# A hybrid pooling and state-space block on one core: the TensorE order of the gate and pooling projections is written out as 64 steps

## The chip, the core and the metric

The kernel runs on one core of a Trainium2 chip. The metric is the device time of one execution in microseconds (us). Before the change the median of three runs is 1359.53 us (1359.49 to 1359.74).

The engines are called as in the profile: PE is the matrix engine (TensorE), PEld its weight loads, DVE the vector engine, ACT the scalar engine with its table functions, POOL the third elementwise engine, SP the engine that issues most DMAs. Each engine runs its own list of instructions in order and waits on semaphores for the others.

## The reference

One layer of a decoder. Two request groups share the weights: 256 prompt tokens and 8 x 4 sample tokens, so 288 columns (N) everywhere. D_MODEL is 2048, that is 16 blocks of 128 (KT).

```python
mod = silu(c) @ w_ada + b_ada                  # six parts: sh1, sc1, g1, sh2, sc2, g2
h = rmsnorm(x, norm1) * (1 + sc1) + sh1
u_pool, z, xbc, dt_raw = split(h @ w_in)       # widths 512, 1536, 2560, 24
pool_out = pool_mixer(u_pool)                  # trailing windows 2/4/8/16, then a 128x128 map per group
ssd_out = ssd_mixer(z, xbc, dt_raw)            # conv of width 4, chunked scan, y * silu(z), rmsnorm
x = x + g1 * (concat([pool_out, ssd_out]) @ w_out)
h2 = rmsnorm(x, norm2) * (1 + sc2) + sh2
x = x + g2 * conv_ffn(h2)                      # gate and value projections, conv of width 3, down projection
y = rmsnorm(x, norm_f)
```

Inside the state-space mixer (SSD) each of four groups has six heads of 64 channels and a state of 128:

```python
Lm = exp(where(mask, cs[l] - cs[s], -inf))                    # decays, per head
y_diag = (C B^T * Lm) @ xdt;  y_off = (C * exp(cs)) @ h_start
chunk_states = (B * decay_to_end)^T @ xdt
```

## The kernel before

Activations are kept transposed, 128 features by 288 tokens a tile. Every large projection is done in three matmuls for one block of weights (`mm3`, lines 295 to 297): the weights are cast on ACT into a rounded high part (`whi`), DVE subtracts to get the low part (`wlo`), and PE adds high x high, high x low and low x high. These matmuls use all 128 columns of the PE array and stream 288 columns; the text calls them **wide**. The wide names are `xbc`, `mm_uz`, `mm_out`, `mm_up`, `mm_gate`, `mm_val` and `mm_down`.

The weights come as one stream of tiles of up to 512 KB, loaded by SP in the order in which the program asks for them into eight `raw` buffers (`RAW0`).

Three kinds of PE work use only part of the array's columns at a time, the text calls them **narrow**: the conditioning matmuls `adap` (32 columns each, four side by side, line 324), `yo` (32 columns) and the SSD outputs `y` (64 columns, two side by side, lines 807 to 817). A float32 matmul stands as two records in the trace, so 8 matmuls of `adap` are 16 records.

The stage that the change is about is the projection of the gate z and of two pooling groups, `uz_units(m)` for eight tiles m. A tile is 16 blocks of the contraction; `project_units` yields every two of them (`YK`), so the stage has 64 steps of six wide matmuls. Between the steps other work is pulled from generators:

- `adas` is the conditioning for parts 2, 3 and 4 of `mod`. One unit of `ada_part_units` (`AY` = 2 blocks) needs four weight tiles and eight `adap` matmuls. The text calls that a **visit**. After a part's eight visits come a copy on ACT (`asb`) and four transposes (`adat`).
- `back` is the SSD. `ssd_group(g)` transposes tokens (`xt`, `bt`), forms C B^T (`cb`), chunk states (`s`), the sample part `yo`, and then for each of three head pairs t the decays `decays(t)` (two matmuls `cse`, six relus and two exps on ACT, one exp over both heads, two products on DVE) and `outputs(t)` (ten matmuls `y`, then DVE and ACT). `conv_group(g)` is the convolution of the next group, 15 DVE operations and a SiLU.
- `late` and `pool_units` are the pooling mixer, `y_norm` the norm of the SSD output: column sums `ysum`, a square root on ACT, a reciprocal on DVE, the matmuls `pbrstdy`, and three products on DVE and one on POOL over the four `zy` tiles.

`pull(gn, rate)` adds the rate to a credit and takes a unit from the generator for every whole credit. In this stage the rates are 0.2 visits and one SSD unit a step. What is pulled is only traced there: the framework's scheduler then orders each engine's instructions by its own estimates, so a visit or a group of `y` may be cut and wide matmuls put between its parts. The block `in_order(...)` (it adds a dependence from each instruction to the one before on the named engines) is used before the change only for the first stage of the kernel.

PSUM for `xt`, `bt`, `cb`, `s`, `yo`, `cse`, `y`, `pool` and `adat` comes from four `aux` banks in turn.

After the stage follows the output projection `mm_out`. Its right-hand sides `mixh` and `mixl` are made on ACT and DVE from the normed `zy` and the pooling output; the first tile can go no faster than they appear.

Of the kernel before, what the change touches and what calls it, by code (L numbers as in the profile page):

```python
# [18 lines left out]
P = 128  # L19
# [31 lines left out]
GB = 4  # L51
AY = 2

RA1, RA2, RB1, RB2, RB3 = 0.5, 0.4, 1.0, 1.0, 1.0
TA, ADA_OUT = 4, 4
TK = 4
GA = (2, 3)
XM = (0, 2, 5, 9)
SM0 = 10
# [102 lines left out]
def kernel(ctx: ExitStack, tc, ins, outs):  # L162
# [14 lines left out]
    def aux(name):  # L177
        return px.tile([P, 512], F32, tag="aux", name=name)
# [80 lines left out]
    def load(key):  # L259
        off, cols = S.items[key]  # L260
        t = wp[0].tile([P, RAWC], F32, tag="raw", name="raw_" + "_".join(map(str, key)))
        nc.sync.dma_start(t[:, :cols], wflat[off:off + P * cols].rearrange("(p n) -> p n", p=P))
        return t
# [54 lines left out]
        return ps  # L318


    def ada_mm(ps, raw, k, c0, nb, js):
        for j in js:
            c = c0 + (j - js[0]) * nb
            nc.tensor.matmul(ps[32 * j:32 * j + 32, :nb], sc_c[:, k, :], raw[:, c:c + nb],  # L324
                             start=(k == 0), stop=(k == KT - 1), tile_position=(0, 32 * j))

    def ada_sb(ps, nb, name, r=P):
        asb = kp.tile([P, 512], F32, tag="asb", name="asb_" + name)
        nc.scalar.copy(asb[0:r, :nb], ps[0:r, :nb])
# [66 lines left out]

    def ada_part_units(part, ay=1):
        ps = pa.tile([P, 512], F32, tag="ada", name=f"adap{part}")
        for k in range(KT):
            raws = [load(("adap", part, k, h)) for h in range(2)]  # L400
            for h in range(2):
                ada_mm(ps, raws[h], k, 0, 512, range(2 * h, 2 * h + 2))
            if k % ay == ay - 1:
                yield
        asb = ada_sb(ps, 512, f"p{part}")
        yield
        pt = ada_tr(asb, 512, f"p{part}")
        for i in range(4):
            o = ada[:, part].rearrange("p (j i) c -> p j i c", j=4)[:, :, i, :]
            b = bada[:, part].rearrange("p (j i) -> p j i", j=4)[:, :, i]  # L410
            src = pt[:, i * P:(i + 1) * P].rearrange("p (j c) -> p j c", j=4)[:, :, 0:NC9]
            nc.vector.tensor_tensor(o, src, b.unsqueeze(2).to_broadcast([P, 4, NC9]), ALU.add)
        if part == 4:
            ada_scale(1, 4, vec[:, V_N2:V_N2 + KT], 0, KT)
        yield
# [237 lines left out]
    def drain(gen):  # L653
        for _ in gen:
            pass
# [54 lines left out]
    def ssd_group(g):  # L710
# [35 lines left out]
        nc.gpsimd.dma_start(sbx[q, P:P + G6], xde[0:NS, 2, :])  # L746
        yield

        s1 = sx[0].tile([P, G6], F32, tag="s1", name=f"s1_{g}")
        ps1 = aux(f"s1_{g}")  # L750
        nc.tensor.matmul(ps1[:, :G6], bt[:, 0, :], xde[:, 0, :], start=True, stop=True)
# [24 lines left out]
                                py[:, :G6].rearrange("p (h q) -> p h q", h=HG),  # L776
                                bc64(dtr["ecs4"][:, hs]), ALU.mult)
        yield

        csr, cs = dtr["csr"], dtr["cs"]  # L780

        def decays(t):

            e = sx[0].tile([P, 2, N], F32, tag="e", name=f"e{g}_{t}", bufs=2)
            ec = sx[0].tile([P, 2, P], F32, tag="ec", name=f"ec{g}_{t}", bufs=2)
            for i in range(2):
                hh = HG * g + 2 * t + i
                pe = aux(f"cse{hh}")
                nc.tensor.matmul(pe[:, :N], selr[:, hh:hh + 1].to_broadcast([P, P]), csr, start=True, stop=True)


                for c in range(3):
                    n = slice(c * P, min(c * P + P, N))
                    nc.scalar.activation(e[:, i, n], pe[:, n], AF.Relu, bias=cs[:, c, hh:hh + 1], scale=-1.0)
                nc.scalar.activation(ec[:, i, :], pe[:, P:NP], AF.Exp)
            nc.scalar.activation(e, e, AF.Exp, scale=-1.0)
            nc.vector.tensor_tensor(e, e, cb.unsqueeze(1).to_broadcast([P, 2, N]), ALU.mult)
            nc.vector.tensor_tensor(ec, ec, cf[:, 4, P:NP].unsqueeze(1).to_broadcast([P, 2, P]), ALU.mult)
            return e, ec

        def outputs(t, e, ec):
            assert (g, t) in zdone
            pq = aux(f"y{g}_{t}")
            rows = [slice(0, 64), slice(64, P)]
            for i, r in enumerate(rows):
                f = slice(64 * (2 * t + i), 64 * (2 * t + i) + 64)
                nc.tensor.matmul(pq[r, NP:N], yo[:, f], seli, start=True, stop=False)
            for i, r in enumerate(rows):
                f = slice(64 * (2 * t + i), 64 * (2 * t + i) + 64)
                nc.tensor.matmul(pq[r, NP:N], xdt[:, 2, f], e[:, i, NP:N], start=False, stop=True)  # L810
            for i, r in enumerate(rows):
                f = slice(64 * (2 * t + i), 64 * (2 * t + i) + 64)
                nc.tensor.matmul(pq[r, 0:P], xdt[:, 0, f], e[:, i, 0:P], start=True, stop=True)
            for i, r in enumerate(rows):
                f = slice(64 * (2 * t + i), 64 * (2 * t + i) + 64)
                nc.tensor.matmul(pq[r, P:NP], xdt[:, 1, f], e[:, i, P:NP], start=True, stop=False)
                nc.tensor.matmul(pq[r, P:NP], s1[:, f], ec[:, i, :], start=False, stop=True)
            yt = cf[:, t, 0:N]
            nc.vector.scalar_tensor_tensor(out=yt, in0=yt,
                                           scalar=vec[:, V_D + 3 * g + t:V_D + 3 * g + t + 1],  # L820
                                           in1=pq[:, :N], op0=ALU.mult, op1=ALU.add)
            zt = zy[g][:, t, :]
            nc.vector.tensor_tensor(zt, zt, yt, ALU.mult)
            sq = kp.tile([P, N], F32, tag="xsq", name=f"ysq{g}_{t}", bufs=2)
            nc.scalar.activation(sq, zt, AF.Square)
            if g + t == 0:
                nc.gpsimd.tensor_copy(ssq, sq)
            else:
                nc.gpsimd.tensor_tensor(ssq, ssq, sq, ALU.add)

        if g < ZEARLY:
            nc.scalar.activation(zy[g], zy[g], AF.Silu)
        dec = [decays(0)]
        yield
        dec.append(decays(1))
        outputs(0, *dec[0])
        yield
        dec.append(decays(2))
        outputs(1, *dec[1])
        yield  # L840
        outputs(2, *dec[2])
# [61 lines left out]
    def chain(*gens):  # L903
        for gn in gens:
            yield from gn
# [50 lines left out]
    def zip2(a, b):  # L956
        a, b = iter(a), iter(b)
        live = 2
        while live:
            live = 0  # L960
            for gn in (a, b):
                try:
                    next(gn)
                    live += 1
                    yield
                except StopIteration:
                    pass

    def h0s(g):
        load_h0(g)  # L970
        yield

    def take(gn, n):
        for _ in range(n):
            next(gn)
            yield

    ssd3 = ssd_group(3)
    back = chain(conv0, h0s(0), zip2(ssd_group(0), conv_group(1)), h0s(1),
                 zip2(ssd_group(1), conv_group(2)), h0s(2), zip2(ssd_group(2), conv_group(3)), h0s(3),  # L980
                 zip2(take(ssd3, TK), chain(pool_units(UEARLY[0]), pool_units(UEARLY[1]))))
    credit = {}

    def pull(gn, rate):

        credit[id(gn)] = credit.get(id(gn), 0.0) + rate
        while credit[id(gn)] >= 1:
            credit[id(gn)] -= 1
            next(gn, None)
# [29 lines left out]
                pull(back, 0.5 if m < 20 else RB1) if m >= 9 else None  # L1019
                pull(adas, RA1 / AY)  # L1020

    late = {}
    n = 0
    zlast = 3 * (4 - ZEARLY) * KT // YK
    for m in list(range(4 + 3 * ZEARLY, 16)) + ULATE:
        for _ in uz_units(m):
            n += 1
            for gn in late.values():
                pull(gn, 0.5)
            pull(adas, RA2 / AY)  # L1030
            pull(back, RB2 if n <= zlast else RB3)
            if n == zlast:
                drain(back)
                back = chain(ssd3, y_norm())
        if m < 4:
            late[m] = pool_units(m)
            next(late[m])
    pull(adas, TA / AY)
    for h, (_, n) in enumerate(_halves(KT)):
        ready[("out", 0, h)] = split(load(("out", 0, h)), 0, n * P, f"out_0_{h}")  # L1040
    for gn in late.values():
        drain(gn)
    drain(back)
    npl = kp.tile([P, 4, 135], F32, tag="hmod", name="npl", bufs=2)
    nc.gpsimd.tensor_copy(npl[:, :, 0:15], upp[:, :, NP:15 + NP])
    nc.gpsimd.tensor_copy(npl[:, :, 15:135].rearrange("p g (b l) -> p g b l", b=NB), ups[:, :, :, 4:19])
# [63 lines left out]
    for m in range(16):  # L1110
        if m in XM:
            sl = slice(4 * XM.index(m), 4 * XM.index(m) + 4)
            nc.sync.dma_start(x[:, sl, :], ins["x"][:, sl, :])
        if m == 5:
            wp[0].add(w2, RAW2, SPLIT2)
        for i, ps in enumerate(project_units(("out", m), KT, order=MIXK)):
            if m == KT - 1 and i == 5:
                all_but_last("ssum2")
        residual(ps, 2, m)
        squares(m, "a")  # L1120
        pull(adas, (1 + (m >= 14 - ADA_OUT)) / AY)
        if m == 13:
            drain(adas)

# [286 lines left out]
```

## Time and profile before

| | |
|---|---|
| median of 3 runs | 1359.53 us |
| the profiled execution's own time | 1359.61 us |
| its span, first to last instruction | 1357.8 us |
| mean granted PE clock | 0.997 |
| PE busy in the span | 1342.5 us, 99% |
| first `mm_dt` matmul | 186.3 us |
| first `mm_uz` matmul | 260.93 us |
| first `mm_out` matmul | 380.34 us |

All times on the trace are us from the start of the span. A matmul is recorded with its full latency, so a wide one shows about 0.30 us though the next starts 0.13 us later; what a matmul takes of PE's time is the distance from its start to the next start. PE shows as busy nearly always, also where it streams at a lower pace, so its busy share doesn't tell how much could be gained. ACT and DVE records overlap a little as well.

### The profile page before, as it was taken

Reading aid. Unit: us, or ns where it says so; the run is one execution under the profiler, and the core shown is the slowest. Engines: PE = TensorE matmul, PEld = TensorE weight load, DVE = VectorE, ACT = ScalarE, POOL = GpSimd, SP = SyncE. Lnnn points to the kernel's source line nnn. Section 1 sums busy time; section 2 is a strip of 40 time slices with the busy share of each in tenths; the row PEclk is TensorE's granted clock in tenths of the full one; section 3 lists DMA queues with packets and bytes.
Section 4 is the critical chain, followed back from the end, with each engine's and each line's share of the span. In section 5 each row is a group of like instructions: output and inputs, shape, how many; then the busy total and the mean of one; then the engine's idle time right before and its main releaser. Section 6 shows DMA issues by size and latency. Waiting matters only on the chain.

```text
span 1357.8 us, 26226 instructions
## 1 busy us (share of the span) xinstructions
PE 1342.5 (99%) x10557; PEld 1247.4 (92%) x10557; DVE 810.1 (60%) x1349; ACT 578.6 (43%) x908; POOL 221.0 (16%) x428
## 2 busy tenths in 40 slices
PE   9999999999999999999999999999999999999997
PEld 7889988776779889999999999999999999999996
DVE  5775568778564448645565455656654556566543
ACT  5243234587643335534443334443433344434442
POOL 0000002122221213111221001212220011222221
PEclk9999999999999999999999999999999999999998
DMA  9999668877888877777555455555554555555531
GB/s 378 405 408 355 252 216 323 335 263 288 326 302 334 310 265 257 248 293 265 184 182 184 167 176 185 197 193 182 189 178 167 183 191 185 192 200 194 180 117 71
DMA packets 97338, 323.20 MB, mean 238 GB/s; under 512 B 10752, under 2 KB 19904, under 8 KB 97216
## 3 DMA queue, kind: packets, MB, share of 16 engines
q1 hardware_dynamic: 93312, 310.64, 62.8%
q0 software_dynamic: 3184, 9.69, 1.9%
q8 instruction: 83, 1.36, 0.4%
q10 hardware_dynamic: 720, 1.19, 0.2%
q14 instruction: 39, 0.32, 0.1%
HBM read 309.78 MB, written 10.39 MB: 236 GB/s over the span
## 4 chain that ended last, share of the span: by engine, by line
PE 96%; DVE 2%; DMA 1%; ACT 0%; issue 0%; SPq 0%; POOL 0%; DVEq 0%; POOLq 0%; ACTq 0%
PE mm_down L296 7%; PE mm_down L295 7%; PE mm_down L297 7%; PE mm_val L296 6%; PE mm_gate L296 6%; PE mm_gate L295 6%; PE mm_gate L297 6%; PE mm_val L297 6%; PE mm_val L295 6%; PE xbc L295 5%; PE adap L324 5%; PE xbc L296 4%; PE xbc L297 4%; PE mm_out L295 3%; PE mm_out L296 3%; PE mm_out L297 2%
## 5 line engine op out<-in xcount | busy, mean ns | idle before, releaser
L296 PE MATMUL mm_down<-al,whi_down 128*128 128x288 f32 x688 | 202.9, 295 | 0.0
L295 PE MATMUL mm_down<-ah,whi_down 128*128 128x288 f32 x688 | 202.7, 295 | 0.0
L297 PE MATMUL mm_down<-ah,wlo_down 128*128 128x288 f32 x688 | 202.4, 294 | 0.0
L296 PE MATMUL mm_gate<-h2l,whi_gate 128*128 128x288 f32 x640 | 189.1, 296 | 0.0
L296 PE MATMUL mm_val<-h2l,whi_val 128*128 128x288 f32 x640 | 189.1, 295 | 0.0
L297 PE MATMUL mm_val<-h2h,wlo_val 128*128 128x288 f32 x640 | 188.8, 295 | 0.0
L297 PE MATMUL mm_gate<-h2h,wlo_gate 128*128 128x288 f32 x640 | 188.8, 295 | 0.0
L295 PE MATMUL mm_gate<-h2h,whi_gate 128*128 128x288 f32 x640 | 188.7, 295 | 0.0
L295 PE MATMUL mm_val<-h2h,whi_val 128*128 128x288 f32 x640 | 187.9, 294 | 0.0
L283 DVE TENSOR_TENSOR wlo_gate<-raw_gate,whi_gate 128x1024 fp32r<-128x1024 f32 x80 | 97.8, 1225 | 135.4 <-ACT whi_gate L281 135.2
L283 DVE TENSOR_TENSOR wlo_down<-raw_down,whi_down 128x1024 fp32r<-128x1024 f32 x96 | 107.5, 1119 | 116.1 <-ACT whi_down L281 115.0
L281 ACT CAST whi_down<-raw_down 128x1024 fp32r<-128x1024 f32 x96 | 92.4, 962 | 167.3 <-PE mm_down L296 118.0
L281 ACT CAST whi_gate<-raw_gate 128x1024 fp32r<-128x1024 f32 x80 | 83.9, 1051 | 159.5 <-PE mm_gate L296 67.7
L281 ACT CAST whi_val<-raw_val 128x1024 fp32r<-128x1024 f32 x80 | 84.1, 1051 | 126.0 <-issue 103.1
L295 PE MATMUL xbc<-h1h,whi_xbc 128*128 128x288 f32 x448 | 133.0, 301 | 1.2 <-ACT h1h L445 1.2
L296 PE MATMUL xbc<-h1l,whi_xbc 128*128 128x288 f32 x448 | 132.1, 296 | 0.0
L297 PE MATMUL xbc<-h1h,wlo_xbc 128*128 128x288 f32 x448 | 130.8, 297 | 0.0
L295 PEld LDWEIGHTS mm_down<-ah,whi_down 128*128 128x128 f32 x688 | 129.3, 188 | 0.0
L296 PEld LDWEIGHTS mm_down<-al,whi_down 128*128 128x128 f32 x688 | 129.3, 188 | 0.0
L297 PEld LDWEIGHTS mm_down<-ah,wlo_down 128*128 128x128 f32 x688 | 129.1, 188 | 0.0
L295 PEld LDWEIGHTS mm_gate<-h2h,whi_gate 128*128 128x128 f32 x640 | 120.5, 188 | 5.0 <-ACT ah L1176 3.4
L295 PEld LDWEIGHTS mm_val<-h2h,whi_val 128*128 128x128 f32 x640 | 120.5, 188 | 0.0
(323 smaller groups left out, 2979.3 us busy)
## 6 DMA issues: line engine op xcount, KB each, us to landing
raw_adap<-wflat SPq DMA_DIRECT2D x128, 512.0 KB, 5.5
raw_gate<-wflat SPq DMA_DIRECT2D x80, 512.0 KB, 3.5
raw_val<-wflat SPq DMA_DIRECT2D x80, 512.0 KB, 3.6
raw_ada<-wflat SPq DMA_DIRECT2D x64, 512.0 KB, 9.7
raw_xbc<-wflat SPq DMA_DIRECT2D x51, 512.0 KB, 8.9
raw_down<-wflat SPq DMA_DIRECT2D x48, 512.0 KB, 3.5
raw_out<-wflat SPq DMA_DIRECT2D x32, 512.0 KB, 6.6
raw_down<-wflat SPq DMA_DIRECT2D x32, 384.0 KB, 3.0
```

The source lines that it names most:

```text
L281: yield nc.scalar.copy(hi[:, :n], raw[:, a:a + n])
L283: yield hi, lo, nc.vector.tensor_tensor(lo[:, :n], raw[:, a:a + n], hi[:, :n].bitcast(F32), ALU.subtract)
L295: nc.tensor.matmul(ps, whi[:, w], bh, start=first, stop=False)
L296: nc.tensor.matmul(ps, whi[:, w], bl, start=False, stop=False)
L297: nc.tensor.matmul(ps, wlo[:, w], bh, start=False, stop=last)
L324: nc.tensor.matmul(ps[32 * j:32 * j + 32, :nb], sc_c[:, k, :], raw[:, c:c + nb], start=(k == 0), stop=(k == KT - 1), tile_position=(0, 32 ...
```

## The change

The generator rates of the stage go, and a plan takes their place: a list of what is pulled at which of the 64 steps. PE's instructions of the stage are put into `in_order`, so that PE has them as they are written. A visit's loads are all asked for first, and its matmuls are tied to each other from the last loaded tile on. In `ssd_group` the decays of the first head pair are made before the chunk states, each group's ten `y` matmuls are written as pairs over the two column halves, and the decays `e` and `ec` get a third buffer. Visits in the output projection are pulled at 5/7 a tile. What is computed stays the same.

```diff
-RA1, RA2, RB1, RB2, RB3 = 0.5, 0.4, 1.0, 1.0, 1.0
-TA, ADA_OUT = 4, 4
-TK = 4
+RA1, RB1 = 0.5, 1.0
+TA, ADA_OUT = 2, 5 / 7
+SSD0 = 4
+GA0, GP, GS = -6, 15, (0, 2, 3, 5, 6, 9, 12, 15)
+GCV, GH0 = (1, 2, 3, 4, 5, 6), 9
+VU = (3, 4, 6, 9, 18, 24, 33, 39, 48, 54, 61)
+YN = (58, 60)
+PU = (24, 28, 33, 34, 36, 39)
+PL = (58, 62)
...
     def ada_part_units(part, ay=1):
         ps = pa.tile([P, 512], F32, tag="ada", name=f"adap{part}")
-        for k in range(KT):
-            raws = [load(("adap", part, k, h)) for h in range(2)]
-            for h in range(2):
-                ada_mm(ps, raws[h], k, 0, 512, range(2 * h, 2 * h + 2))
-            if k % ay == ay - 1:
-                yield
+        for ka in range(0, KT, ay):
+            raws = [(k, h, load(("adap", part, k, h))) for k in range(ka, ka + ay) for h in range(2)]
+            tied = False
+            for k, h, raw in raws[::-1]:
+                for j in (2 * h, 2 * h + 1):
+                    with tc.high_priority() if tied else nullcontext():
+                        i = nc.tensor.matmul(ps[32 * j:32 * j + 32, :512], sc_c[:, k, :],
+                                             raw[:, (j % 2) * 512:(j % 2) * 512 + 512],
+                                             start=(k == ay - 1), stop=(k == KT - ay), tile_position=(0, 32 * j))
+                    if tied:
+                        tc.keep_in_program_order(i)
+                    tied = True
+            yield
...
+            e = sx[0].tile([P, 2, N], F32, tag="e", name=f"e{g}_{t}", bufs=3)
+            ec = sx[0].tile([P, 2, P], F32, tag="ec", name=f"ec{g}_{t}", bufs=3)
...
+            prods = [(P, NP, lambda i: (s1[:, fs[i]], ec[:, i, :]), True, False),
+                     (P, NP, lambda i: (xdt[:, 1, fs[i]], e[:, i, P:NP]), False, True),
+                     (0, P, lambda i: (xdt[:, 0, fs[i]], e[:, i, 0:P]), True, True),
+                     (NP, N, lambda i: (xdt[:, 2, fs[i]], e[:, i, NP:N]), True, False),
+                     (NP, N, lambda i: (yo[:, fs[i]], seli), False, True)]
+            for n0, n1, ops, first, last in prods:
+                for i, r in enumerate(rows):
+                    nc.tensor.matmul(pq[r, n0:n1], *ops(i), start=first, stop=last)
...
+    for g in range(4):
+        if g:
+            for i in range(3 if g == 1 else 0, 6):
+                at(GA0 + GP * (g - 1) + GCV[i], convs[g])
+            at(GA0 + GP * (g - 1) + GH0, h0s(g))
+        for i in range(SSD0 if g == 0 else 0, 8):
+            at(GA0 + GP * g + GS[i], ssds[g])
+    for n in VU:
+        at(n, adas)
+    for gn, steps in ((early_pool, PU), (yn, YN), (late[ULATE[0]], PL)):
+        for n in steps:
+            at(n, gn)
...
+    with in_order(nc.tensor.engine):
+        n = 0
+        step(0)
+        for m in list(range(4 + 3 * ZEARLY, 16)) + ULATE:
+            for _ in uz_units(m):
+                n += 1
+                if n % (KT // YK):
+                    step(n)
+            if m < 4:
+                next(late[m])
+            step(n)
+    pull(adas, TA)
```

**PE, the first tile of the stage.** The rows of before run from the second half of the visit with weight tiles 14 and 15 of part 2 through the first and second head pair of group 0 (`y_0`, `y_1`):

```order
L324 MATMUL adap_2522<-raw_adap_14_0_3278,sc_c 32x512 x2
L324 MATMUL adap_2522<-raw_adap_14_1_3280,sc_c 32x512 x2
L324 MATMUL adap_2522<-raw_adap_15_0_3286,sc_c 32x512
L810 MATMUL y_0_3240<-e_0_3190,xdt_2986 64x32 x2
L813 MATMUL y_0_3240<-e_0_3190,xdt_2986 64x128 x2
L816 MATMUL y_0_3240<-e_0_3190,xdt_2986 64x128
L817 MATMUL y_0_3240<-ec_0_3191,s_0_3116 64x128
L324 MATMUL adap_2522<-raw_adap_15_0_3286,sc_c 32x512
L324 MATMUL adap_2522<-raw_adap_15_1_3288,sc_c 32x512 x2
L789 MATMUL cse_3296<-csr,selr 128x288
...
L807 MATMUL y_1_3311<-vec,yo_3140 64x32 x2
L295 MATMUL mm_uz_3176<-h1h_123,whi_uz_1_3268 128x288
```

The same work in the changed kernel, the group `y_0` and the visit with tiles 14 and 15:

```order
L795 MATMUL y_0_3250<-ec_0_3118,s_0_3168 64x128 x2
L795 MATMUL y_0_3250<-e_0_3117,xdt_2986 64x128 x4
L795 MATMUL y_0_3250<-e_0_3117,xdt_2986 64x32 x2
L795 MATMUL y_0_3250<-vec,yo_3192 64x32 x2
L769 MATMUL cse_3268<-csr,selr 128x288
L769 MATMUL cse_3274<-csr,selr 128x288
L409 MATMUL adap_2522<-raw_adap_15_1_3295,sc_c 32x512 x2
L409 MATMUL adap_2522<-raw_adap_15_0_3293,sc_c 32x512 x2
```

The visit is no longer cut by `y_0`, and the product with `yo`, which stood apart from its group, is its last pair. Over the whole program PE's list has, from the first `mm_dt` to the first `mm_up`, 77 unbroken runs of wide matmuls before and 52 after (in the stage itself 48 and 26).

**PE, the norm of the SSD output near the end of the stage.** Before, wide matmuls stand between the column sums and the matmuls that spread the result:

```order
L296 MATMUL mm_uz_4305<-h1l_144,whi_uz_1_4449 128x288
L235 MATMUL ysum<-ones,ssq 128x1 x3
L297 MATMUL mm_uz_4305<-h1h_128,wlo_uz_1_4451 128x288
L295 MATMUL mm_uz_4507<-h1h_113,whi_uz_0_4510 128x288
...
L296 MATMUL mm_uz_4507<-h1l_135,whi_uz_0_4510 128x288
L248 MATMUL pbrstdy<-early,r3rstdy 128x128 x2
L248 MATMUL pbrstdy<-early,r3rstdy 128x32
L297 MATMUL mm_uz_4507<-h1h_119,wlo_uz_0_4512 128x288
```

Left out there are 18 further wide rows of `mm_uz`. In the changed kernel the two follow at once:

```order
L305 MATMUL mm_uz_4474<-h1l_132,whi_uz_0_4477 128x288
L306 MATMUL mm_uz_4474<-h1h_116,wlo_uz_0_4479 128x288
L244 MATMUL ysum<-ones,ssq 128x1 x3
L257 MATMUL pbrstdy<-early,r3rstdy 128x128 x2
L257 MATMUL pbrstdy<-early,r3rstdy 128x32
L304 MATMUL mm_uz_4474<-h1h_117,whi_uz_0_4477 128x288
```

What moved is the wide work that stood between them; it is now ahead and behind.

**ACT, the start of the stage.** Before, the two casts of the first tile's weights, `whi_uz_0` and `whi_uz_1`, stand ahead of all decays:

```order
L281 CAST whi_uz_0_3179<-raw_uz_0_3177 128x1024
L832 ACTIVATE zy_150<-zy_150 128x864
L281 CAST whi_uz_1_3268<-raw_uz_1_3266 128x1024
L794 ACTIVATE e_0_3190<-cse_3192,csd 128x128 x2
L794 ACTIVATE e_0_3190<-cse_3192,csd 128x32
L795 ACT_TABLE_LOAD
L795 ACTIVATE ec_0_3191<-cse_3192 128x128
```

In the changed kernel the second cast stands behind the decays of the second head pair (`e_1`, the rows before these) and inside those of the third (`e_2`):

```order
L776 ACTIVATE e_1_3194<-e_1_3194 128x576
L695 ACT_TABLE_LOAD
L695 ACTIVATE cf_3020<-cf_3020 128x5x32
L803 ACTIVATE ysq_0_3263<-zy_149 128x288
L774 ACTIVATE e_2_3266<-cse_3268,csd 128x128 x2
L290 CAST whi_uz_1_3315<-raw_uz_1_3313 128x1024
L774 ACTIVATE e_2_3266<-cse_3268,csd 128x32
L775 ACT_TABLE_LOAD
```

ACT's list has 20 table loads before and 28 in the changed kernel, because exps and SiLUs alternate more often; between the first `mm_uz` and the square root of the norm there are 14 before and 19 after.

More of the change, by code (lines that the diff above doesn't have):

```diff
@@ L318, in project @@
         return ps
[L321 to L325, printed above, removed]
     def ada_sb(ps, nb, name, r=P):
@@ L747, in ssd_group, with decays @@
         yield
+        csr, cs = dtr["csr"], dtr["cs"]
+        def decays(t):
+            e = sx[0].tile([P, 2, N], F32, tag="e", name=f"e{g}_{t}", bufs=3)
+            ec = sx[0].tile([P, 2, P], F32, tag="ec", name=f"ec{g}_{t}", bufs=3)
+            for i in range(2):
+                hh = HG * g + 2 * t + i
+                pe = aux(f"cse{hh}")
+                nc.tensor.matmul(pe[:, :N], selr[:, hh:hh + 1].to_broadcast([P, P]), csr, start=True, stop=True)
+                for c in range(3):
+                    n = slice(c * P, min(c * P + P, N))
+                    nc.scalar.activation(e[:, i, n], pe[:, n], AF.Relu, bias=cs[:, c, hh:hh + 1], scale=-1.0)
+                nc.scalar.activation(ec[:, i, :], pe[:, P:NP], AF.Exp)
+            nc.scalar.activation(e, e, AF.Exp, scale=-1.0)
+            nc.vector.tensor_tensor(e, e, cb.unsqueeze(1).to_broadcast([P, 2, N]), ALU.mult)
+            tc.keep_in_program_order(nc.vector.tensor_tensor(
+                ec, ec, cf[:, 4, P:NP].unsqueeze(1).to_broadcast([P, 2, P]), ALU.mult))
+            return e, ec
@@ new lines, in outputs @@
+        def outputs(t, e, ec):
+            assert (g, t) in zdone
+            pq = aux(f"y{g}_{t}")
+            rows = [slice(0, 64), slice(64, P)]
+            fs = [slice(64 * (2 * t + i), 64 * (2 * t + i) + 64) for i in range(2)]
+            prods = [(P, NP, lambda i: (s1[:, fs[i]], ec[:, i, :]), True, False),
[6 more added lines that the diff above has]
+                    nc.tensor.matmul(pq[r, n0:n1], *ops(i), start=first, stop=last)
+            yt = cf[:, t, 0:N]
+            nc.vector.scalar_tensor_tensor(out=yt, in0=yt,
+                                           scalar=vec[:, V_D + 3 * g + t:V_D + 3 * g + t + 1],
+                                           in1=pq[:, :N], op0=ALU.mult, op1=ALU.add)
+            zt = zy[g][:, t, :]
+            nc.vector.tensor_tensor(zt, zt, yt, ALU.mult)
+            sq = kp.tile([P, N], F32, tag="xsq", name=f"ysq{g}_{t}", bufs=2)
+            nc.scalar.activation(sq, zt, AF.Square)
+            if g + t == 0:
+                nc.gpsimd.tensor_copy(ssq, sq)
+            else:
+                nc.gpsimd.tensor_tensor(ssq, ssq, sq, ALU.add)
@@ L749, in ssd_group @@
+        if g < ZEARLY:
+            nc.scalar.activation(zy[g], zy[g], AF.Silu)
+        dec = [decays(0)]
+        yield
         s1 = sx[0].tile([P, G6], F32, tag="s1", name=f"s1_{g}")
@@ L778, in ssd_group @@
         yield
[L780 to L829, printed above, removed]
@@ L831, in ssd_group @@
-        if g < ZEARLY:
-            nc.scalar.activation(zy[g], zy[g], AF.Silu)
-        dec = [decays(0)]
+        dec.append(decays(1))
         yield
-        dec.append(decays(1))
         outputs(0, *dec[0])
+        dec.append(decays(2))
         yield
-        dec.append(decays(2))
         outputs(1, *dec[1])
@@ L976, in take @@
             yield
[L978 to L981, printed above, removed]
+    ssds = [ssd_group(g) for g in range(4)]
+    convs = [conv0] + [conv_group(g) for g in range(1, 4)]
+    back = chain(conv0, h0s(0), zip2(take(ssds[0], SSD0), take(convs[1], 3)))
     credit = {}
@@ L1020, with at, step @@
                 pull(adas, RA1 / AY)
[L1022 to L1038, printed above, removed]
+    drain(back)
+    yn = y_norm()
+    early_pool = chain(pool_units(UEARLY[0]), pool_units(UEARLY[1]))
+    late = {m: pool_units(m) for m in ULATE}
+    plan = [[] for _ in range(4 * KT + 1)]
+    def at(n, gn):
+        plan[max(n, 0)].append(gn)
+    for g in range(4):
[10 more added lines that the diff above has]
+            at(n, gn)
+    def step(n):
+        for gn in plan[n]:
+            next(gn, None)
+    with in_order(nc.tensor.engine):
[10 more added lines that the diff above has]
+    pull(adas, TA)
     for h, (_, n) in enumerate(_halves(KT)):
@@ L1042 @@
         drain(gn)
-    drain(back)
+    drain(yn)
     npl = kp.tile([P, 4, 135], F32, tag="hmod", name="npl", bufs=2)
@@ L1120 @@
         squares(m, "a")
-        pull(adas, (1 + (m >= 14 - ADA_OUT)) / AY)
+        pull(adas, ADA_OUT)
         if m == 13:
```

## The prediction

> **What bounds the kernel now.** I read the page first: busy shares and the chain that ended last.
>
> ```profile
> PE 1342.5 (99%) x10557; PEld 1247.4 (92%) x10557; DVE 810.1 (60%) x1349; ACT 578.6 (43%) x908; POOL 221.0 (16%) x428
> PE 96%; DVE 2%; DMA 1%; ACT 0%; issue 0%; SPq 0%; POOL 0%; DVEq 0%; POOLq 0%; ACTq 0%
> ```
>
> PE sets the time nearly everywhere, so a change pays only if PE streams with fewer losses or waits less. The chain is an average, so next came the view by windows of the stage, first the whole of it, then 15 of its steps (PE, PEld, DVE, ACT, POOL busy, clock, DMA share, GB/s), and PE's waits in the stage.
>
> ```profile
> 261.00:380.30 119.30, 117.57 (x948) 84.65 (x948) 85.35 (x159) 88.71 (x198) 27.64 (x37) 1.00 0.80 296
> 301.20:326.50 25.30, 25.30 (x219) 17.60 (x222) 20.23 (x39) 21.24 (x47) 6.66 (x11) 1.00 0.80 293
> PE pool L877 <- DVE pout L872: 0.7, 1, 0.7
> PE cse L789 <- DVE ada L412: 0.5, 1, 0.5
> PE cb L739 <- DVE xde L728: 0.4, 1, 0.4
> PE ysum L235 <- POOL ssq L829: 0.2, 1, 0.2
> ```
>
> Waits are 1.8 us of 119.3. Clock 1.00 and DMA share 0.80 leave no other bound. But ACT is busy 88.7 us (74%), and 21.2 of 25.3 us (84%) in the middle: a second engine stands close behind. What is left to gain lies in how PE streams, which the timeline of PE shows (start, length, what).
>
> ```profile
> 300.46 0.29 PE L296 MATMUL mm_uz<-h1l,whi_uz 128*128 128x288 f32 x1
> 300.69 0.31 PE L807 MATMUL y<-vec,yo 128*64 128x32 f32 x4
> 300.93 0.40 PE L297 MATMUL mm_uz<-h1h,wlo_uz 128*128 128x288 f32 x1
> 301.17 0.29 PE L295 MATMUL mm_uz<-h1h,whi_uz 128*128 128x288 f32 x1
> 301.30 0.29 PE L296 MATMUL mm_uz<-h1l,whi_uz 128*128 128x288 f32 x1
> ```
>
> From start to start a wide matmul takes 0.13 us (301.17 to 301.30), but 0.23 before a narrow group (300.46 to 300.69) and 0.24 as the first behind one (300.93 to 301.17). **A break costs 0.10 + 0.10 = 0.20 us.**
>
> The second loss is in the visits. The chain of waits shows a whole one and, first and last of eight, cut ones:
>
> ```profile
> 202.71 0.98 PE adap L324 x2
> 208.65 1.85 PE adap L324 x14
> 220.72 1.85 PE adap L324 x16
> ...
> 502.69 0.98 PE adap L324 x2
> 504.44 2.71 PE adap L324 x22
> ```
>
> Whole, 16 records take 1.85 us; cut into 2 and 14 they take 0.98 + 1.85 = 2.83, as much as half a visit more. The last pair holds a visit and a half: 3.69 against 1.5 x 1.85 = 2.78.
>
> **The change part by part.** The sum is made against the profiled execution's 1359.61 us; the median, 1359.53, is practically the same.
>
> *A. Visits tied.* In the new order no visit is cut. Eight times 0.97 = 7.8 us. Nothing hides this, since PE has no idle time there.
>
> *B. Fewer breaks.* The order has 52 unbroken wide runs between the first `mm_dt` and the first `mm_up`, against 77: 25 x 0.20 = 5.0. Some narrow kinds (`ysum`, the transposes) may cost less than the `y` group that I measured, so I take 4.5 (bounds 3 and 5).
>
> *C. The `y` groups.* Rows of a group without the product with `yo` and of one with it, each with the wide matmul behind:
>
> ```profile
> 307.63 0.31 PE L810 MATMUL y<-e,xdt 128*64 128x32 f32 x4
> ...
> 308.60 0.40 PE L295 MATMUL mm_uz<-h1h,whi_uz 128*128 128x288 f32 x1
> 353.26 0.31 PE L807 MATMUL y<-vec,yo 128*64 128x32 f32 x4
> ...
> 353.52 0.42 PE L813 MATMUL y<-e,xdt 128*64 128x128 f32 x4
> 353.77 0.44 PE L816 MATMUL y<-e,xdt 128*64 128x128 f32 x4
> ...
> 354.35 0.40 PE L295 MATMUL mm_uz<-h1h,whi_uz 128*128 128x288 f32 x1
> ```
>
> In two places a group takes 0.97 (307.63 to 308.60) + 0.24 (300.69 to 300.93) = 1.21, in one 1.09 (353.26 to 354.35): 0.12 x 11 groups = 1.3. Within it the eight records that alternate badly between the halves (353.77 to 354.35) take 0.58, where two well-paired fours would take 2 x 0.25 (353.52 to 353.77): up to 0.08 x 12 = 1.0, at least nothing. I take 1.0, since the pair in the row is the same shape. Together 2.3.
>
> *D. Waits gone.* `pool`, `cse` and `cb` stand later behind their producers in the new order: 0.7 + 0.5 + 0.4 = 1.6.
>
> Gains: 7.8 + 4.5 + 2.3 + 1.6 = **16.2 us**.
>
> Against them stands that PE is now in written order: while its next instruction waits, everything behind it waits, on PE and then on ACT and DVE, which wait for PE's banks.
>
> *E. The start of the stage.* The cast of `whi_uz_1` moves behind the decays. A row of PE's chain, ACT's timeline, one of DVE's and a group of ACT's price what is ahead of it:
>
> ```profile
> 255.92 1.43 PE yo L771 x16
> ...
> 255.96 0.48 ACT L760 COPY s<-s 128x384 f32<-128x384 f32 x1
> 256.34 1.05 ACT L281 CAST whi_uz<-raw_uz 128x1024 fp32r<-128x1024 f32 x1
> ...
> 262.15 0.80 ACT L794 ACTIVATE e<-cse,csd 128x128 f32<-128x128 f32 x3 [0.62 <-PE cse L789]
> 262.96 1.28 ACT L795 ACT_TABLE_LOAD   x1
> 264.25 0.28 ACT L795 ACTIVATE ec<-cse 128x128 f32<-128x128 f32 x1
> ...
> 265.85 0.81 ACT L794 ACTIVATE e<-cse,csd 128x128 f32<-128x128 f32 x3
> 261.56 1.23 DVE L283 TENSOR_TENSOR wlo_uz<-raw_uz,whi_uz 128x1024 fp32r<-128x1024 f32 x1 [0.79 <-ACT whi_uz L281]
> L682 ACT ACTIVATE cf<-cf 128x1280 f32<-128x1280 f32 x2 | 2.6, 1282 | 0.0
> ```
>
> Let T be the start of the first `mm_uz`. ACT's list, from the first state copy (about T - 1.7: `yo`'s 1.43 and two `cse`, 0.3 by the pace of wide matmuls, stand between) to the end of that cast: copy 0.48, table load 1.28, SiLU 1.28, copy 0.48, the pair `e_1` 3.70 (262.15 to 265.85, with its load), load 1.28, small SiLU and square 0.75 (an estimate), two relus 0.55, cast 1.05: 10.85, so it ends at T + 9.15. DVE's low part, 1.23, ends at T + 10.4. PE comes there after 24 wide (3.2), `y_0` (1.1), two `cse` (0.3), a visit (1.85) and a break: T + 6.7 for the high part and T + 6.95 for the low. PE waits about **3.5 us**. Bounds: 0, if ACT has done the convolution's SiLU before T and the squares don't hold it up; 6, if ACT also waits for `y_0`'s products, or if the visit's loads, which SP now has behind state loads, come late too.
>
> *F. The norm.* `ysum` and `pbrstdy` are now neighbours, and wide work no longer covers what lies between.
>
> ```profile
> 367.60 0.83 PE L235 MATMUL ysum<-ones,ssq 128*128 128x1 f32 x6 [0.18 <-POOL ssq L829]
> 371.15 0.75 PE L248 MATMUL pbrstdy<-early,r3rstdy 128*128 128x128 f32 x6
> 368.52 1.28 ACT L241 ACT_TABLE_LOAD   x1
> 369.81 0.26 ACT L241 ACTIVATE r3rstdy<-ysum,epst 128x3 f32<-128x3 f32 x1
> 370.11 0.18 DVE L242 RECIPROCAL r3rstdy<-r3rstdy 128x3 f32<-128x3 f32 x1
> ```
>
> The sums end at 368.43, the reciprocal at 370.29: 1.9, plus a hand-over to PE, 2.3 at most. In the list the load itself waits for nothing, and the square root behind it does; loaded early, 0.26 + 0.18 and three hand-overs remain, 0.7. I take 1.0, near the lower end.
>
> *G. The seam.* `mixl` is the last thing that the first `mm_out` tile needs.
>
> ```profile
> 389.59 0.82 DVE L1053 TENSOR_TENSOR mixl<-pout,mixh 128x288 fp32r<-128x288 f32 x2
> ```
>
> DVE's chain took 371.15 to 390.41, 19.3 us; one `wlo` and small products fewer make about 17.5. PE has, from `pbrstdy` to the end of that tile, 84 wide (11.1), two visits (3.7) and an estimated 1.4 of pooling matmuls and transposes (two groups like `pbrstdy`'s 0.75): 16.2. So it waits 1.3 (0 to 2.5).
>
> *H. The middle.* If the stage shrinks to some 107 us, ACT with five table loads more (19 for 14) has 88.7 + 5 x 1.28 = 95 us, 89%. The trace shows no such stage; by the rows above, in which ACT at 84% costs PE nothing, the price could be nil, and if each added load lands on PE's path, 6.4. I take 1.5.
>
> Costs: 3.5 + 1.0 + 1.3 + 1.5 = 7.3. Net 16.2 - 7.3 = 8.9: 1359.6 - 8.9 = **1350.7 us**.
>
> One rule would say otherwise. The Trainium skill, "ScalarE: Activation LUTs", section "What ACT_TABLE_LOAD costs", adds to a load of about 1283 ns a drain of about 1380 ns. The load agrees with the row at 262.96; the drain doesn't show: relus end at 262.95, the load starts at 262.96 and the exp at 264.25. By that rule 19 loads would add 26 us to ACT and the stage couldn't shrink; the row decides.
>
> **The rivals.**
>
> 1. *The waits vanish.* ACT's and DVE's queues adapt, and E to H cost 0 to 3 us: 1343.4 to 1346.5. For it: 1.8 us of waits now. Against: E follows from the list.
> 2. *ACT becomes the bound.* Its 95 us hold hand-overs that must alternate with PE; added loads on the path (6.4) in place of H's 1.5, with the upper values of E or F, leave a net gain of 0 to 5: 1354.6 to 1359.6. For it: 84% in the middle already.
> 3. *Slower: every `y` group waits for its decays.* From `cse` to the products ACT takes 3.7 and DVE about 1.2 (the row below); the plan puts six steps, 6/15 of 25.3 = 10.1 us, between `cse` and `y`.
>
> ```profile
> L797 DVE TENSOR_TENSOR e<-e,cb 128x576 f32<-128x576 f32 x12 | 9.0, 753 | 0.4
> ```
>
> So a group waits only when ACT and DVE run over 5 us behind. Before, PE would slip wide work in; in order it can't. With E to G at 5.8, the point is (16.2 - 5.8)/12 = 0.87 us a group; at 1.2 to 1.5 us the time is 1363 to 1367. Against: the third buffer lets the decays run ahead.
> 4. *The order doesn't come about*, because visits wait for weights: DMA share 0.80 speaks against it; it would land with rival 2.
>
> **How the numbers follow.** Forecast (a net gain of 5 to 13, 1346.5 to 1354.6) 0.54; rival 1 0.14; rivals 2 and 4 0.23; rival 3 0.09. A measurement of this kernel can tell about 0.2%, 2.7 us, from no change: faster ends at 1356.8. Half of rivals 2 and 4 lies above it, so faster 0.54 + 0.14 + 0.11 = 0.79, same 0.12, slower 0.09. The range leaves out the better half of rival 1, a tip of rival 2 and all of rival 3: 1344.5 to 1358.5.
>
> **What would show it.** A: `adap` only in rows of x16 or whole multiples. B and C: `y` in one piece of about 1.0 us. E: PE waiting for `whi_uz` or `wlo_uz` within 10 us of the first `mm_uz`; F: a wait at `pbrstdy` of 0.7 to 2.3; G: waits of `mm_out` for `mixl`. H, or rivals 2 and 3: waits of `y`, `cse` or `mm_uz` for ACT and DVE all through the stage, adding up to over 5 us, would make the forecast wrong; if all waits together stay under 3, rival 1 holds.

## The result, and the profile after

| | before | changed |
|---|---|---|
| median | 1359.83 us (6 runs, 1359.49 to 1360.14) | 1367.59 us (6 runs, 1366.33 to 1369.77) |
| span of the profiled execution | 1357.8 us | 1365.1 us |

The ratio is 1.006, with a 95% interval of 1.0049 to 1.007: the change made the kernel **7.8 us slower**, where 8.9 us faster was forecast. The page's busy shares and chain of the changed kernel:

```profile
PE 1333.9 (98%) x10557; PEld 1248.3 (91%) x10557; DVE 811.7 (59%) x1349; ACT 589.1 (43%) x916; POOL 221.3 (16%) x428
PE 91%; DMA 3%; DVE 3%; ACT 2%; issue 1%; SPq 0%; DVEq 0%; ACTq 0%
```

PE is busy 8.6 us less than before, and the span is longer all the same: PE holds 91% of the chain now, not 96%, and DMA, DVE and ACT hold the rest. Where the time went shows in windows of three stretches (the stage, `mm_out` up to the first `mm_up`, and `mm_up`; columns as before). First the kernel before:

```profile
260.90:380.30 119.40, 117.67 (x952) 84.73 (x948) 85.35 (x159) 88.81 (x198) 27.64 (x37) 1.00 0.80 295
380.30:507.10 126.80, 126.39 (x948) 109.03 (x945) 58.83 (x100) 43.98 (x63) 25.67 (x39) 1.00 0.80 307
507.10:545.40 38.30, 38.30 (x291) 38.24 (x289) 32.42 (x58) 20.85 (x37) 12.14 (x19) 1.00 0.77 264
```

And the changed kernel:

```profile
262.40:381.20 118.80, 107.17 (x930) 83.61 (x929) 84.69 (x157) 93.50 (x195) 29.43 (x38) 0.99 0.77 283
381.20:513.10 131.90, 126.86 (x964) 109.16 (x962) 59.80 (x102) 46.41 (x66) 27.63 (x42) 1.00 0.84 314
513.10:553.10 40.00, 40.00 (x289) 39.80 (x290) 31.87 (x57) 19.28 (x35) 9.76 (x20) 0.96 0.69 240
```

The stage lost only 0.6 us, though PE is busy 10.5 us less in it; `mm_out` became 5.1 us longer (one visit of 1.85 moved there), `mm_up` 1.7 us longer at a clock of 0.96. Another 1.3 us is gone before the first `mm_dt`, where PE, ACT and SP have the same instructions in the same order in both kernels: the first `xbc` starts at 20.57 us, in twelve of the other thirteen profiles of this study at 19.0 to 19.6, in one at 20.61. That part comes and goes from run to run.

PE's waits, in the stage and then from the first `mm_out` on:

```profile
PE y L795 <- DVE ec L778: 4.0, 2, 3.4
PE y L795 <- DVE yo L840: 2.5, 1, 2.5
PE pbrstdy L257 <- DVE pout L883: 1.7, 1, 1.7
PE adap L409 <- DMA raw_adap<-wflat: 1.6, 1, 1.6
PE adat_p L338 <- ACT asb_p L332: 0.8, 1, 0.8
PE mm_uz L306 <- DVE wlo_uz L292: 0.7, 1, 0.7
PE yo L836 <- issue: 0.2, 1, 0.2
```
```profile
PE mm_up L304 <- ACT h2h L456: 2.3, 1, 2.3
PE adap L409 <- DMA raw_adap<-wflat: 1.9, 1, 1.9
PE mm_out L306 <- DVE wlo_out L292: 0.7, 1, 0.7
```

Before, the stage had 1.8 us of waits. Added up from start to start of PE's records (a distance over 0.56 us counts 0.25 as work and the rest as waiting), the stage divides like this, with the best kernel of the experiments beside it:

| us in the stage | before | changed | `n_ta3` |
|---|---|---|---|
| wide matmuls and breaks | 58.6 | 54.8 | 56.4 |
| visits | 23.1 (10) | 16.7 (9) | 18.5 (10) |
| `y` | 14.7 | 13.2 | 12.8 |
| other narrow work | 21.0 | 21.9 | 19.5 |
| waits | 2.0 | 12.2 | 3.2 |
| sum | 119.4 | 118.8 | 110.3 |

**The gains of A, B and C came; waits took them back.** The longest one, on ACT's timeline of the changed kernel (the third head pair of group 2):

```profile
324.85 0.80 ACT L774 ACTIVATE e<-cse,csd 128x128 f32<-128x128 f32 x3 [1.46 <-PE cse L769]
325.65 1.28 ACT L775 ACT_TABLE_LOAD   x1
326.95 0.28 ACT L775 ACTIVATE ec<-cse 128x128 f32<-128x128 f32 x1
327.24 1.28 ACT L693 ACT_TABLE_LOAD   x1
328.54 1.28 ACT L693 ACTIVATE cf<-cf 128x1280 f32<-128x1280 f32 x1
...
331.31 0.79 ACT L774 ACTIVATE e<-cse,csd 128x128 f32<-128x128 f32 x3
332.11 1.28 ACT L775 ACT_TABLE_LOAD   x1
333.40 0.28 ACT L775 ACTIVATE ec<-cse 128x128 f32<-128x128 f32 x1
333.58 0.68 ACT L776 ACTIVATE e<-e 128x576 f32<-128x576 f32 x1
```

Exp for one head, the convolution's SiLU, exp for the other: three table loads inside one pair. Left out between them are a cast of weights, a second, small SiLU and a square. From the first relu to the last exp it takes 9.4 us (324.85 to 334.26); the twelve pairs of the kernel before took 2.4 to 5.1. DVE's products follow, and PE, which may not put anything in between, stands still for 3.36 us, to 336.82.

The next longest, 2.5 us for `yo`, is on DVE's timeline. PE stands still until 324.17, and ahead of the product `yo` DVE has operations of the convolution, one of the pooling and a `wlo`:

```profile
318.98 2.66 DVE L683 SCALAR_TENSOR_TENSOR cf<-cvp,vec,cf 128x312 f32<-128x312 f32 x4
321.56 0.41 DVE L878 SCALAR_TENSOR_TENSOR pout<-pp,upp 128x256 f32<-128x256 f32 x1
321.90 1.21 DVE L292 TENSOR_TENSOR wlo_uz<-raw_uz,whi_uz 128x1024 fp32r<-128x1024 f32 x1
323.04 0.53 DVE L683 SCALAR_TENSOR_TENSOR cf<-cvp,vec,cf 128x312 f32<-128x312 f32 x1
...
323.57 0.54 DVE L840 TENSOR_TENSOR yo<-yo,ex 128x384 f32<-128x384 f32 x1
```

Windows around the longest wait and around the first `mm_up` show a second price:

```profile
335.00:337.00 2.00, 0.17 (x2) 0.18 (x4) 1.97 (x5) 0.25 (x1) 1.16 (x1) 0.99 0.17 70
337.00:340.40 3.40, 3.40 (x29) 3.31 (x27) 1.45 (x5) 0.00 (x0) 0.00 (x0) 0.50 0.00 0
340.40:344.00 3.60, 3.60 (x28) 1.89 (x27) 2.90 (x7) 0.57 (x2) 1.30 (x2) 1.00 0.31 109
511.00:514.40 3.40, 1.30 (x8) 1.10 (x9) 2.23 (x6) 1.50 (x3) 0.91 (x3) 1.00 0.99 389
514.40:517.80 3.40, 3.40 (x16) 3.40 (x16) 2.39 (x6) 0.84 (x2) 1.60 (x4) 0.51 1.04 409
```

Behind each of these two waits the granted clock is 0.50 for 3.41 us. That costs 1.7 us each time, twice in this execution; behind the wait for `yo` it stays at 1.00.

### The profile page after: what moved, and what is told of

The parts are those of the page before. It is cut to its first block, busy times and chain, and to the rows that moved or that the text cites. A ratio compares the mean times of both kernels' runs of the same rounds, so it can differ in the third digit from the quotient of the medians.

```text
span 1365.1 us, 26218 instructions
## 1 busy us (share of the span) xinstructions
PE 1333.9 (98%) x10557; PEld 1248.3 (91%) x10557; DVE 811.7 (59%) x1349; ACT 589.1 (43%) x916; POOL 221.3 (16%) x428
## 4 chain that ended last, share of the span: by engine, by line
PE 91%; DMA 3%; DVE 3%; ACT 2%; issue 1%; SPq 0%; DVEq 0%; ACTq 0%
PE mm_down L305 7%; PE mm_down L304 7%; PE mm_down L306 7%; PE mm_val L305 6%; PE mm_gate L305 6%; PE mm_gate L304 6%; PE mm_val L306 6%; PE mm_gate L306 6%; PE mm_val L304 6%; PE xbc L304 4%; PE xbc L306 4%; PE xbc L305 4%; PE adap L409 4%; PE mm_out L304 2%; PE mm_out L306 2%; PE mm_out L305 2%
```

## The experiments

The theory: the streaming gains are real, but PE in written order turns each lateness of ACT, DVE or DMA into idle time. The rivals: the gains never came; the plan overloads ACT and DVE in any order; the loss lies outside the stage. The kernel before ran beside them at 1359.5 to 1359.6 us.

| run | from, and edit | median us | ratio to before (95%) |
|---|---|---|---|
| `a_noorder` | changed, no `in_order` | 1356.31 | 0.9976 (0.9966 to 0.9985) |
| `a_seam` | changed, last part untied | 1364.16 | 1.0039 (1.0025 to 1.0053) |
| `b_tied` | before, tied visits | 1358.44 | 0.9991 (0.9982 to 1.0001) |
| `b_ypairs` | before, `y` pairs | 1362.94 | 1.0026 (1.0016 to 1.0035) |
| `a_decpin` | changed, decays tied on ACT | 1360.50 | 1.0005 (0.9995 to 1.0014) |
| `n_ta2` | `a_noorder` + `a_seam` | 1353.86 | 0.9956 (0.9941 to 0.9971) |
| `n_ta3` | `n_ta2`, one visit earlier | **1351.53** | 0.9942 (0.9927 to 0.9957) |
| `n_bufs2` | `n_ta2`, two decay buffers | 1353.99 | 0.9960 (0.9946 to 0.9974) |
| `n_dec` | `n_ta3` + `a_decpin` | 1353.18 | 0.9953 (0.9940 to 0.9965) |
| `o_dec` | `n_dec` with `in_order` | 1359.15 | 1.0003 (0.9988 to 1.0018) |
| `n_oldy` | `n_ta3`, old `y` order | 1354.74 | 0.9965 (0.9952 to 0.9979) |
| `n_untied` | `n_ta3`, old visits | 1361.11 | 1.0016 (1.0007 to 1.0025) |

**`a_noorder`.** The scheduler may order PE's list again.

```diff
-    with in_order(nc.tensor.engine):
+    with nullcontext():
```

> The changed kernel with only the in_order block around the 64 steps taken away; plan, tied visits, y pairs and third buffers stay. Theory W (the gains came, but PE, now in written order, waits for ACT and DVE lists in the stage: about 12 us of gaps from the first mm_uz to the first mm_out): the scheduler can again put wide matmuls into the waits, PE's waits in the stage fall from about 12 us to under 4, the stage gets shorter than 118.8 us by 4 or more, and the whole lands at 1357 to 1363. Rival P (the plan itself loads ACT and DVE so that PE waits in any order): waits stay above 9 us and the time within 2 us of 1367.6.

11.3 us faster than the changed kernel, and better than expected. The stage takes 108.3 us instead of 118.8, its waits 3.4 instead of 12.2. Theory W holds and rival P falls: the same plan waits little when the scheduler may order PE's list. But ACT's list is another one too: it has 26 table loads instead of 28, and the head pair that took 9.4 us takes 5.5. So this run alone doesn't part what PE fills in from what ACT saves; `o_dec` against `n_dec`, further down, does it better. What is left of the forecast is lost behind the stage: a visit waits 3.2 us for its weights, with half a clock behind it, and `mm_up` waits 1.5 us for `h2h`.

**`a_seam`.** The last part's visits as before.

```diff
-        for ka in range(0, KT, ay):
+        if part == 5:
+            for k in range(KT):
+                raws = [load(("adap", part, k, h)) for h in range(2)]
+                for h in range(2):
+                    ada_mm(ps, raws[h], k, 0, 512, range(2 * h, 2 * h + 2))
+                if k % ay == ay - 1:
+                    yield
+        else:
```

> The changed kernel with the old, untied visits for the last part (5) alone. Theory S (tying that part's loads moves a weight cast that waits for its DMA ahead of the two h2h casts on ACT; PE waits before the first mm_up, and the long wait is followed by 3.4 us at half clock): the wait for h2h of 2.3 us and the half-clock stretch behind it vanish, and the time falls by 3 to 4 us, to about 1364. Rival: the late weights hold the seam up anyway; within 1 us of 1367.6.

3.4 us faster, as expected, and the wait for `h2h` is gone from the list. ACT's timeline of the changed kernel shows the cause: a cast of weights that waits 2.38 us for its DMA stands ahead of the two `h2h` casts.

```profile
511.88 0.83 ACT L290 CAST whi_upk<-raw_upk 128x768 fp32r<-128x768 f32 x1 [2.38 <-DMA raw_upk<-wflat]
512.62 0.76 ACT L456 CAST h2h<-h_n 128x288 fp32r<-128x288 f32 x2
```

**`b_tied`.** `ada_part_units` of the change in the kernel before, the last part excepted.

> The kernel before with only the tied visits of parts 2 to 4 (the last part keeps the old form). Theory A (a cut visit costs PE 0.97 us more than a whole one, eight of them): minus 6 to minus 8 us, to 1352 to 1354, and the stage from the first mm_uz to the first mm_out about 4 to 5 us shorter. Rival (a whole visit must wait for its last loaded tile and holds PE up, or the cut filled idle time): within 2 us of 1359.8.

Only 1.1 us, and not certain: the forecast of theory A missed, and the number is the one that the rival gave. The visits did get shorter (18.5 us for ten in the stage instead of 23.1), and the first `mm_out` starts at 375.04 instead of 380.34. But there PE then waits for what had been hidden:

```profile
PE pool L893 <- DVE pout L888: 2.1, 2, 1.2
PE mm_out L296 <- DVE mixl L1076: 1.9, 1, 1.9
```

and two stretches at half clock, 6.83 us from 378.8 on, take 3.4 more. Theory A holds for the matmuls; the time was given back at the seam.

**`b_ypairs`.** The change's five pairs in the kernel before.

> The kernel before with only the ten y matmuls of a head pair written as five pairs over the two column halves, yo last. Theory C (eight records that stay on one half cost 0.08 us a group, the apart product 0.12 and a break of 0.2): minus 1 to minus 4 us, depending on whether the scheduler now keeps a group in one piece. Rival: within 0.5 us of 1359.8.

A miss: 3.4 us slower. The `y` records in the stage take 13.3 us instead of 14.7, so C holds there. But the scheduler's order moved as well: visits are cut in more places (24.4 us instead of 23.1), and `mm_out` waits 2.4 us for `mixl` with 1.7 of half clock behind it. A gain in one part alone is no measure of it where a scheduler answers.

**`a_decpin`.** Nothing may stand between the ACT operations of a head pair.

```diff
+        def pin(tied, op):
+            with tc.high_priority() if tied else nullcontext():
+                i = op()
+            if tied:
+                tc.keep_in_program_order(i)
...
-                nc.scalar.activation(ec[:, i, :], pe[:, P:NP], AF.Exp)
-            nc.scalar.activation(e, e, AF.Exp, scale=-1.0)
+                pin(1, lambda: nc.scalar.activation(ec[:, i, :], pe[:, P:NP], AF.Exp))
+            pin(1, lambda: nc.scalar.activation(e, e, AF.Exp, scale=-1.0))
```

The relus are pinned in the same way, but for the first.

> The changed kernel (with in_order), only the scalar-engine operations of a head pair's decays tied to each other, so that no SiLU and no table load of another kind stands between them (22 table loads in ACT's list instead of 28). Theory W1 (the 3.4 us wait of the last y group of group 2 comes from exp, SiLU and exp loads inside its decays): that wait falls below 1 us, the half-clock stretch behind it goes (1.7 us), and the time falls by 3 to 6 us, to 1362 to 1364. Rival W2 (DVE's queue, not ACT's, is late for the products): the wait stays above 2 us, time within 1.5 us of 1367.6.

7.1 us faster than the changed kernel, more than the 3 to 6 expected, and the wait of `y` for `ec` is gone. W1 holds for the wait. Where the whole 7.1 us came from stays open: the profile is of an execution of 1362.54 us, 2.0 above the median, which has four stretches at half clock at other places. What stays in its stage are waits for DVE and DMA, the longest of them:

```profile
PE y L801 <- DVE yo L846: 2.9, 1, 2.9
PE adap L409 <- DMA raw_adap<-wflat: 1.9, 1, 1.9
PE pbrstdy L257 <- DVE pout L889: 1.7, 1, 1.7
```

**`n_ta2`, `n_ta3`, `n_bufs2`.** `n_ta2` joins the edits of `a_noorder` and `a_seam`; the other two start from it.

```diff
-TA, ADA_OUT = 2, 5 / 7
+TA, ADA_OUT = 3, 9 / 14
```
```diff
-            e = sx[0].tile([P, 2, N], F32, tag="e", name=f"e{g}_{t}", bufs=3)
+            e = sx[0].tile([P, 2, N], F32, tag="e", name=f"e{g}_{t}", bufs=2)
```

(`ec` likewise in `n_bufs2`.)

> Without the in_order block and with the old visits for the last part: the two single edits together. If their gains add: 1356.3 less the 1.5 us wait for h2h before the first mm_up, so 1354 to 1355.5; if the wait only moves, 1356 to 1357.

> As n_ta2, but the visit that waited 3.2 us for its weights at the start of mm_out is asked for ahead of the first mm_out weights (three units after the stage instead of two, 9/14 a tile after it). Theory D (its loads stand behind those of mm_out on SP): the wait and the half-clock stretch behind it go, minus 3 to 5 us against n_ta2, so 1350 to 1352. Rival M (the seam is bound by the chain norm, zy, mixl on DVE): PE then waits there for mixl, 1 to 3 us, and the gain is under 2 us.

> As n_ta2, with two buffers of the decays e and ec instead of three. Theory B (third buffers let decays run ahead and are worth something where PE must wait): 1 to 3 us slower than n_ta2, with waits of y or cse. Rival: within 0.7 us of n_ta2.

`n_ta2` at 1353.86, 13.7 us faster than the changed kernel: the gains of 11.3 and 3.4 add, but for 1.0. `n_ta3` at 1351.53 is the best of all, 16 us faster than the changed kernel and 8 us than before. D and M are both in it: the wait for weights and the half clock go, but PE now waits 1.3 us for `mixl`, so the gain is 2.3 us, less than D alone would have given. Its waits from the stage's start to `mm_gate` are few:

```profile
PE mm_out L305 <- DVE mixl L1105: 1.3, 1, 1.3
PE pool L901 <- DVE pout L896: 1.1, 1, 1.1
PE adap L423 <- DMA raw_adap<-wflat: 0.9, 1, 0.9
PE y L809 <- DVE yo L854: 0.6, 1, 0.6
PE y L809 <- DVE ec L792: 0.2, 1, 0.2
PE mm_out L306 <- DVE wlo_out L292: 0.2, 1, 0.2
PE mm_uz L306 <- DVE wlo_uz L292: 0.2, 1, 0.2
```

`n_bufs2` is at 1353.99, the same as `n_ta2`: without the written order the third buffers are worth nothing.

**`n_dec`, `o_dec`.** Three of the causes mended (ACT's decays, the late visit, the last part), without and with the written order.

> n_ta3 with the scalar-engine operations of a pair's decays tied as in a_decpin (20 table loads in ACT's list instead of 26). If ACT's switching still costs PE anything without the written order, minus 1 to 2 us against n_ta3 (1351.5), through the waits of y and of pool; if the scheduler already fills those waits, within 0.7 us.

> n_dec with the in_order block put back: written order on PE, but ACT's decays tied, the late visit asked for early, the last part untied. Theory W (the written order turns every lateness of ACT, DVE or DMA into idle PE time, and idle time of more than about half of a 3.4 us window into 1.7 us more): waits in the stage stay at 8 us or more, and it is 4 to 9 us slower than n_dec, 1355 to 1360. Rival (with those causes mended the written order is as good or better, since it has fewer breaks, 55 wide runs for 65): within 1.5 us of n_dec or faster.

`n_dec` is 1.7 us slower than `n_ta3`, which neither guess had: its stage is 0.8 us shorter in the profile, and `mm_out` 1.9 longer. So tying ACT's operations helps here only with the written order. `o_dec` is 6.0 us slower than `n_dec` and varies from 1356.8 to 1366.2. Its stage is 120.9 us long, that of `n_dec` 109.5. Its waits from the stage's start to `mm_gate`:

```profile
PE y L815 <- DVE yo L860: 2.9, 1, 2.9
PE adap L423 <- DMA raw_adap<-wflat: 1.9, 1, 1.9
PE pbrstdy L257 <- DVE pout L903: 1.7, 1, 1.7
PE pool L907 <- DVE pout L902: 1.6, 2, 0.8
PE adat_p L344 <- ACT asb_p L338: 0.6, 1, 0.6
```

Together 8.7 us, and 13.65 us of the program ran at half clock, so 6.8 us more are lost. With ACT's pairs tied in both (22 table loads here, 20 in `n_dec`), the written order itself is the cause; mending some of its waits leaves the rest.

**`n_oldy`, `n_untied`.** The gains taken away one by one from the best kernel.

> n_ta3 with the ten y matmuls in the old order (yo first, the two column halves badly alternated in the last eight records). Theory C: the y records take about 2 us more in the stage, and the time is 1 to 2.5 us above n_ta3. Rival: no change, within 0.7 us.

> n_ta3 with all visits in the old, untied form; the order has six cut visits from the first mm_dt on. Theory A: 6 x 0.97 = 5.8 us more matmul time, part of it in place of waits at the seam: 3 to 6 us above n_ta3. Rival: within 1.5 us.

Without the pairs it is 3.2 us slower: the `y` records take 14.1 us instead of 12.8 in the stage, and the rest came as waits in `mm_out`. Without tied visits it is 9.6 us slower: ten visits take 23.5 us instead of 18.5 in the stage. Its profile, of an execution of 1363.03 us, has 2.7 us more ahead of the first `mm_dt`, the part that comes and goes, and 3.0 more from the first `mm_out` to the first `mm_up`. Both gains are real. In the matmuls they are a little under what was expected (1.3 of 2 us, 5.0 of 5.8); in the whole time both came out above the expected ranges (1 to 2.5 and 3 to 6), with the rest in other places, in `mm_out` above all.

## Why the prediction failed

- **A, B, C: right, a little large.** From the first `mm_dt` to the first `mm_up`, counted as in the table, visits take 48.8 us instead of 56.4: 7.6 of the 7.8 forecast. The stage's table has 3.8 less in wide matmuls and breaks (4.5 forecast for the program; the trace has 80 and 54 wide runs, not 77 and 52), and 1.5 less in `y`, 1.9 in `n_ta3` (2.3 forecast). That nothing hides A's gain was wrong for the kernel before: in `b_tied` waits at the seam took it back.
- **D: right.** The three small waits are not in the list any more.
- **E: right in size (3.5), half right in cause.** Measured 1.6 + 0.8 + 0.7 = 3.1. `whi_uz_1` was cast and `wlo_uz_1` made 7.2 to 9.5 us after the first `mm_uz` (8.1 to 10.4 in the working). But PE never waited for the cast: it first waited 1.6 us at the visit, for weights whose load SP had behind state loads. The prediction named that as a bound.
- **F: 1.0 forecast, 1.7 measured,** within its bounds. The load wasn't early, since ACT had copies ahead of it, and the reciprocal stood behind pooling products on DVE.
- **G: wrong place.** In the changed kernel `mixl` is never late, since a visit in the first tile waits 1.9 us for its weights instead. In `n_ta3` it is late by 1.3 us, the number forecast; that is luck, since the working was for the written order and another place of that visit.
- **H: the step that failed.** 1.5 us forecast; the waits of `y` and `yo` are 4.0 + 2.5 + 0.2 = 6.7 us. The mechanism is that of rival 3, but at three places and not in every group: ACT's list put the convolution's SiLU inside a pair's decays (3.4 us of the 4.0; `a_decpin` shows it), and DVE's put a `wlo` and convolution operations ahead of `yo` (read from its list alone, no run moved them). ACT's load was about what H foresaw, 93.5 us busy in the stage for 95. What failed is the price put on it: the rows "in which ACT at 84% costs PE nothing" are of a kernel whose PE list the scheduler ordered. There six of the twelve pairs had other operations inside as well, and no wait of `y` is among PE's. The working averaged over the stage, where 15-step sums left room; the waits come from the order inside one pair, which ACT's list shows row by row. Only the start of the stage was read that way. The sign that the prediction gave for this, waits of `y`, `cse` or `mm_uz` of over 5 us together, came, though at single places and not all through the stage: 4.0 + 2.5 + 0.7 = 7.2. That the time, 1367.6, lies next to rival 3's 1363 to 1367 is luck, since over half of the distance came from elsewhere, as the sum below shows.
- **Not in the sum:** the half clock behind long waits, 2 x 1.7 = 3.4 us; the seam at `mm_up`, 1.8 us (9.15 from the last `mm_out` to the first `mm_up`, before 7.30), from tied visits of the last part, a part of the program the prediction didn't follow.

The distance between forecast and profile is 8.9 + 7.3 = 16.2 us. H explains 5.2, the half clock 3.4, the seam 1.8, the start of the program 1.3, F 0.7, the waits in `mm_out` another 1.3 (2.6 for G's 1.3), and E gives 0.4 back: 13.3. The other 2.9 us are mostly gains that came out smaller (B by 0.7, C by 0.8, A by 0.2) and narrow work that took 0.9 longer; the half-clock stretch at 337 lies in these rows too, so they weren't told apart further.

## What to carry to other kernels

An engine's written order removes breaks, but it also removes what hid every late operand; tie what must stay together (here visits and pairs) and leave the scheduler free to put other work into the waits. Before an in-order list is costed by sums, each consumer in it is to be set against its producer's own list, row by row, looking for foreign operations between the parts. And where the bound engine gets faster, the next seam is priced with it: `b_tied` lost nearly all of a 5 us gain there.

## What the runs showed of the hardware

Idle time of PE costs more than its length, and the threshold is lower than I thought. In fourteen profiles the clock's changes inside the program lie on a grid of 3.41 us (in the changed kernel the two starts, 337.0 and 514.5, are 52.0 steps apart). Counted by PE's records in the grid's steps, all fourteen steps with 1.84 us or more of idle time were followed by a step at half clock; of eight with 1.60 to 1.83 four were; below 1.60 none was, but for two steps that were at half clock themselves (0.89 us in `b_tied`, 0.41 in `o_dec`). The end of each program, where its matmuls run out, is not counted. So the same wait costs 1.7 us more or nothing, by where it falls: the wait for `yo` (2.5 us) puts 1.61 us of idle time into one step in the changed kernel and has no half clock behind it, and 1.69 us in `a_seam`, where it has. That the kernels with long waits vary more from run to run fits only in part: the changed kernel varies from 1366.3 to 1369.8, `o_dec` by 9 us, and `n_ta3`, which has no such step, by 0.6; but `n_bufs2`, with a wait of 2.8 us, varies by 1.0, and `n_oldy`, without such a step in its profile, by 2.8. The Trainium skill, "TensorE: Matmul & The Clock Gate", section "HAM oscillation — how this bites in real kernels", warns of idle gaps over some 3.4 us; here the trace shows that shorter ones do it too.
